# Split tokens and split weights in tiles that begin at many different byte offsets

## The chip, the cores and the metric

The kernel runs on 1 core of one Trainium2 chip. The metric is device time in microseconds (us) of one execution, from the program's start to its end. Before the change it is 2146.31 us, the median of 3 runs (2145.34 to 2146.55).

## What is computed

The reference is the trunk of an encoder with two layers, 256 tokens and a model width of 2048, all in float32. Cut to what matters here, one layer is

```
h = rms_norm(x, ln1_g)
qa, ka, va, qb, kb, vb = split(h @ w_in)          # 2048 -> 4608
oa = neighborhood_attention(qa, ka, va, rpb)      # 8 heads of 128
ob = windowed_gqa_sink(qb, kb, vb, sink)          # 8 heads, 2 key heads
x = x + concat(rms_norm(oa), rms_norm(ob)) @ w_out
h2 = rms_norm(x, ln2_g)
u = depthwise_conv(h2 @ w_up)                     # 2048 -> 2 * 5632
x = x + (silu(u[:5632]) * u[5632:]) @ w_down      # 5632 -> 2048
```

Nearly all of the arithmetic is in the four large products with w_in, w_out, w_up and w_down.

## The kernel before, in words

**Products of split numbers.** TensorE multiplies in a 32-bit format that is rounded (fp32r in the profile). To keep float32 accuracy each number is written as the sum of a rounded high part and a low part (`split`, lines 95 to 104: ScalarE writes the high part in L98 or L101, VectorE the rest in L99 or L102), and three partial products are added: high by high, low by high, high by low. So tokens and weights lie in SBUF as pairs of tiles.

- Split tokens: `xs[k]`, k from 0 to 15, each 128 partitions by 2 parts by 256 tokens (2048 bytes in each partition), made by `prep_x` (line 115) from the residual stream; and the tiles named `mid`, of the same shape, which hold the attention outputs (line 366) and the gated activations (line 513).
- Split weights: the pair `whi`, `wlo`, each 128 by 1024 numbers (4096 bytes in each partition), made by `split_w` (line 573).

**Quanta and steps.** The weights arrive by DMA in quanta of 128 by 2048 numbers (1 MB, tile `raw`, three buffers, line 567). Each quantum is two steps of 1024 columns. The loop at the end of the function (lines 662 to 668) goes through all steps in order: it splits the weights four steps ahead (SPLIT_AHEAD), then runs the matmuls of the present step. `whi` and `wlo` have five buffers each, under one name each, in rotation.

**Two forms of product.** For w_in, w_out and w_down (`three`, line 382) the split tokens are the stationary operand (loaded into the array, 128 columns, 512 bytes in each partition) and 512 columns of `whi` or `wlo` stream past. A step has 12 such matmuls: 8 that stream `whi`, 4 that stream `wlo`. The profile names them `mm<-whi,mid`, `mm<-wlo,mid`, `mm<-whi,xs` and `mm<-wlo,xs`: the streamed tile comes first, the stationary one second. For w_up (`two`, line 377) the weights are stationary and the tokens stream: one matmul of 512 columns (both parts of a token tile) against `whi`, `mm<-xs,whi`, and one of 256 columns (the high part) against `wlo`, `mm<-xs,wlo`. A step has 8 such pairs. Every matmul has its own weight load, listed as LDWEIGHTS on PEld, and the load for the next matmul runs beside the present one.

Between them stand smaller float32 matmuls and transposes of the attention, on tiles `qT`, `kT`, `v_a`, `v_b`, `qtok`, `prob`, `prob_a`, and of the residual stream `x`.

**Order.** The Tile framework's scheduler orders each engine's instructions; the split of a step can be done as soon as its `raw` has landed and the buffer that it writes has been read for the last time.

Of the kernel before, what the change touches and what calls it, by code (L numbers as in the profile page):

```python
# [12 lines left out]
F32R = mybir.dt.float32r  # L13
# [5 lines left out]
P = 128  # L19
L = 2  # L20
T = 256
# [20 lines left out]
LOAD_AHEAD = 3  # L42
SPLIT_AHEAD = 4
AHEAD_PRIO = 40


@with_exitstack
def encoder_kernel(
# [7 lines left out]
    wp = ctx.enter_context(tc.tile_pool(name="wp", bufs=2))  # L56
    act = ctx.enter_context(tc.tile_pool(name="act", bufs=1))
# [37 lines left out]
    def split(hi, lo, src, scale=None):  # L95

        if scale is None:
            high = nc.scalar.activation(hi, src, AF.Copy)  # L98
            nc.vector.tensor_sub(lo, src, hi.bitcast(F32))  # L99
        else:  # L100
            high = nc.scalar.activation(hi, src, AF.Copy, scale=scale)  # L101
            nc.vector.scalar_tensor_tensor(lo, src, scale, hi.bitcast(F32),  # L102
                                           op0=ALU.mult, op1=ALU.subtract)
        return high
# [7 lines left out]
    xs = {}  # L112
    st = {}

    def prep_x(l, which, k, src):

        xs[k] = act.tile([P, 2, T], F32R, name=f"xs{k}")
        split(xs[k][:, 0], xs[k][:, 1], src, ln_g[:, which, l, k:k + 1])

    def square_x(nb):  # L120
# [7 lines left out]
    def turn_x(l, which, nb):  # L128

        for k in range(4 * nb, 4 * nb + 4, 2):  # L130
            ps = psum.tile([P, 2, T], F32, name="S", bufs=2)
            for j in range(2):
                for tt in range(TT):
                    nc.tensor.transpose(ps[:, j, tt * P:(tt + 1) * P], x[:, tt, (k + j) * P:(k + j + 1) * P], ident)  # L134
            for j in range(2):
                prep_x(l, which, k + j, ps[:, j, :])
# [305 lines left out]
    def add_x(nb, ps, r=None):  # L442
        xv = x[:, :, nb * 512:(nb + 1) * 512]
        if r is None:
            nc.vector.tensor_add(xv, xv, ps)  # L445
        else:
            for tt in range(TT):
                nc.vector.scalar_tensor_tensor(xv[:, tt], ps[:, tt], r[:, tt:tt + 1], xv[:, tt],
                                               op0=ALU.mult, op1=ALU.add)
# [17 lines left out]
    def whole_x(q, l, which, nb, ps, r=None):  # L467

        with tc.high_priority(offset=4 * AHEAD_PRIO if nb == NB - 1 else 0):
            add_x(nb, ps, r)  # L470
# [7 lines left out]
    def q_up(l, f, u):  # L478
        def body(q, half, hi, lo):
# [8 lines left out]
            if u == 1 and half == 1:  # L488
                with tc.high_priority(offset=4 * AHEAD_PRIO if f == NF - 1 else 0):
                    glu(l, f, ps)  # L490
        return body

    def glu(l, f, ps):
        ux = halo[f % 2]
        r = T // GRID_W
        t = work.tile([P, 2, T], F32, name="prob", bufs=2)
        nc.scalar.activation(t, ps[:, :, 0], AF.Copy)  # L497
        nc.vector.tensor_add(t, t, ps[:, :, 1])  # L498
        nc.vector.tensor_mul(ux[:, :, r:r + T], t, st["r2"][:, None, :].to_broadcast([P, 2, T]))  # L499

        nc.gpsimd.tensor_copy(ux[:, :, 1:r], ux[:, :, T:T + r - 1])  # L501
        nc.gpsimd.tensor_copy(ux[:, :, T + r:T + 2 * r - 1], ux[:, :, r + 1:2 * r])
        y = work.tile([P, 2, T], F32, name="pT", bufs=4)
        for j in range(2):
            c = j * NF + f
            w0, w1, w2, b = (par["conv"][:, l, i, c:c + 1] for i in range(4))
            nc.scalar.activation(y[:, j, :], ux[:, j, r:r + T], AF.Identity, scale=w1, bias=b)  # L507
            for w, o in ((w0, 0), (w2, 2 * r)):
                nc.vector.scalar_tensor_tensor(y[:, j, :], ux[:, j, o:o + T], w, y[:, j, :],  # L509
                                               op0=ALU.mult, op1=ALU.add)  # L510
        nc.scalar.activation(t[:, 0, :], y[:, 0, :], AF.Silu)  # L511
        nc.vector.tensor_mul(t[:, 1, :], t[:, 0, :], y[:, 1, :])  # L512
        gs[f] = act.tile([P, 2, T], F32R, name="mid", bufs=16)
        split(gs[f][:, 0], gs[f][:, 1], t[:, 1, :])
# [22 lines left out]
    for l in range(L):  # L537
# [7 lines left out]
        f = 0  # L545
# [17 lines left out]
    raw, hl, left, loads, highs = {}, {}, {}, {}, {}  # L563

    def load(q, parts=1):
        if q < len(quanta):
            raw[q] = wp.tile([P, 2048], F32, name="raw", bufs=3)
            left[q] = 2
            m = 2048 // parts
            for j in range(parts):  # L570
                loads[q] = nc.sync.dma_start(out=raw[q][:, j * m:(j + 1) * m], in_=quanta[q][0][:, j * m:(j + 1) * m])  # L571

    def split_w(s, parts=1):
        if s < len(steps):
            q, half = steps[s]
            hl[s] = tuple(wp.tile([P, 1024], F32R, name=t, bufs=SPLIT_AHEAD + 1) for t in ("whi", "wlo"))
            m = 1024 // parts
            for j in range(parts):
                with tc.high_priority(offset=AHEAD_PRIO if s >= KD // 2 else 0):
                    highs[s] = split(*(t[:, j * m:(j + 1) * m] for t in hl[s]),  # L580
                                     raw[q][:, half * 1024 + j * m:half * 1024 + (j + 1) * m])
            left[q] -= 1
            if left[q] == 0:
                del raw[q]
                load(q + LOAD_AHEAD)
# [11 lines left out]
    def first_x(i):  # L597
        for j in range(2):
            prep_x(0, 0, 2 * i + j, xT[i][:, j, :])
# [45 lines left out]
    for i in range(SPLIT_AHEAD):  # L645
        first_x(i)
        split_w(i, 2 if i == 0 else 1)
# [14 lines left out]
    for s, (q, half) in enumerate(steps):  # L662
        if s + SPLIT_AHEAD < KD // 2:
            first_x(s + SPLIT_AHEAD)
        split_w(s + SPLIT_AHEAD)
        quanta[q][1](q, half, *hl.pop(s))
        for f, args in side.pop((q, half), []):
            f(*args)
# [83 lines left out]
```

## Time and profile before

| what | value |
|---|---|
| median of 3 runs | 2146.31 us |
| the profiled execution, its own time | 2145.35 us |
| its span, first to last instruction | 2143.6 us |
| mean granted TensorE clock | 0.999 |
| busy: PE, PEld, DVE, ACT, POOL | 2135.8, 1812.2, 1462.1, 1141.5, 66.0 us |
| matmuls | 10896 |
| HBM traffic | 185 GB/s over the span |

Engines are called PE (matmuls of TensorE), PEld (its weight loads), DVE (VectorE), ACT (ScalarE), POOL (GpSimd) and SP (SyncE, which issues the DMAs). A row of a group reads: line, engine, operation, tile written and tiles read, shapes, count | busy us, mean ns of one | idle time just before them, and what ended it. Matmuls are pipelined: the recorded length of one overlaps the start of the next, so lengths don't add up to the span.

### The profile page before, as it was taken

How to read it: one execution, taken by the hardware profiler on the slowest of the kernel's cores; microseconds unless marked ns; L12 is line 12 of the kernel's file. 1: busy time of each engine (PE TensorE's matmuls, PEld its weight loads, DVE VectorE, ACT ScalarE, POOL GpSimd, SP SyncE). 2: the span in 40 equal slices, each digit the busy share in tenths (PEclk: the TensorE clock that was granted, in tenths of full speed). 3: DMA queues.
4: the chain of work that ended last, by engine and by line, in shares of the span. 5: the costliest groups of instructions: out<-in, count | busy, mean ns of one | idle time of the engine just before them, and what ended most of it. 6: DMA issues, size and time to landing. Idle time of an engine off the chain costs nothing.

```text
span 2143.6 us, 28784 instructions
## 1 busy us (share of the span) xinstructions
PE 2135.8 (100%) x10896; PEld 1812.2 (85%) x10896; DVE 1462.1 (68%) x2291; ACT 1141.5 (53%) x1651; POOL 66.0 (3%) x215
## 2 busy tenths in 40 slices
PE   9999999999999999999999999999999999999999
PEld 7888888888888888888888888888888888888887
DVE  7777667775677567657756866677756775776575
ACT  7466556554455355535655665555544553555453
POOL 0000000000000000000000000000000000000000
PEclk9999999999999999999999999999999999999999
DMA  9544555555555555555555344555555555555553
GB/s 340 194 141 167 175 177 177 188 186 197 183 190 191 190 190 179 194 195 178 195 178 196 138 170 164 177 177 184 189 197 180 193 188 187 194 178 196 191 183 137
DMA packets 60555, 397.89 MB, mean 186 GB/s; under 512 B 7296, under 2 KB 9344, under 8 KB 13440
## 3 DMA queue, kind: packets, MB, share of 16 engines
q1 hardware_dynamic: 59840, 395.00, 53.5%
q8 instruction: 85, 1.39, 0.3%
q10 hardware_dynamic: 576, 1.05, 0.2%
q14 instruction: 54, 0.44, 0.1%
HBM read 393.93 MB, written 2.10 MB: 185 GB/s over the span
## 4 chain that ended last, share of the span: by engine, by line
PE 99%; DMA 0%; SPq 0%; DVE 0%; ACT 0%; DVEq 0%; issue 0%
PE mm L80 95%; PE pv L80 1%; PE S L80 1%; PE tr L286 1%; PE S L134 0%; PE tr L347 0%; PE tr L80 0%; DMA raw<-in_w_in 0%; PE tr L342 0%; PE tr L339 0%; DVE x L533 0%; ACT whi L98 0%; DVEq L747 0%; SPq L571 0%; SPq L64 0%
## 5 line engine op out<-in xcount | busy, mean ns | idle before, releaser
L99 DVE TENSOR_TENSOR wlo<-raw,whi 128x1024 fp32r<-128x1024 f32 (+1 forms) x737 | 901.8, 1224 | 558.4 <-ACT whi L98 522.3
L98 ACT ACTIVATE whi<-raw 128x1024 fp32r<-128x1024 f32 (+1 forms) x737 | 779.8, 1059 | 885.8 <-PE mm L80 682.4
L80 PE MATMUL mm<-xs,whi 128*128 128x512 f32 x2816 | 995.0, 399 | 0.0
L80 PE MATMUL mm<-xs,wlo 128*128 128x256 f32 x2816 | 790.9, 281 | 0.0
L80 PEld LDWEIGHTS mm<-xs,whi 128*128 128x128 f32 x2816 | 528.9, 188 | 131.4
L80 PEld LDWEIGHTS mm<-xs,wlo 128*128 128x128 f32 x2816 | 531.9, 189 | 0.7
L80 PE MATMUL mm<-whi,mid 128*128 128x512 f32 x1920 | 481.0, 391 | 0.0
L80 PEld LDWEIGHTS mm<-whi,mid 128*128 128x128 f32 x1920 | 358.0, 188 | 72.8
L80 PE MATMUL mm<-whi,xs 128*128 128x512 f32 x1152 | 297.7, 396 | 2.4 <-ACT whi L98 2.4
L80 PE MATMUL mm<-wlo,mid 128*128 128x512 f32 x960 | 259.3, 390 | 0.0
L80 PEld LDWEIGHTS mm<-whi,xs 128*128 128x128 f32 x1152 | 215.6, 189 | 47.2 <-ACT whi L98 2.9
L80 PEld LDWEIGHTS mm<-wlo,mid 128*128 128x128 f32 x960 | 180.1, 188 | 37.2
L80 PE MATMUL mm<-wlo,xs 128*128 128x512 f32 x576 | 162.0, 396 | 0.0
L509 DVE SCALAR_TENSOR_TENSOR pT<-halo,conv,pT 128x256 f32<-128x256 f32 x352 | 146.4, 475 | 0.1
L80 PEld LDWEIGHTS mm<-wlo,xs 128*128 128x128 f32 x576 | 107.6, 189 | 21.4
L507 ACT ACTIVATE pT<-halo,conv 128x256 f32<-128x256 f32 x176 | 95.0, 587 | 0.0
L499 DVE TENSOR_TENSOR halo<-prob,r 128x512 f32<-128x512 f32 x88 | 60.9, 692 | 2.7
L501 POOL COPY halo<-halo 128x6 f32<-128x6 f32 x88 | 17.7, 201 | 1454.7 <-DVE halo L499 1454.7
L498 DVE TENSOR_TENSOR prob<-prob,mm 128x512 f32<-128x512 f32 x88 | 59.9, 680 | 0.0
L445 DVE TENSOR_TENSOR x<-x,mm 128x1024 f32<-128x1024 f32 x28 | 34.2, 1221 | 35.2 <-PE mm L80 35.2
L497 ACT ACTIVATE prob<-mm 128x512 f32<-128x512 f32 x88 | 51.0, 579 | 0.0
L512 DVE TENSOR_TENSOR prob<-prob,pT 128x256 f32<-128x256 f32 x88 | 36.9, 419 | 1.5 <-ACT prob L511 1.5
(129 smaller groups left out, 840.9 us busy)
## 6 DMA issues: line engine op xcount, KB each, us to landing
raw<-in_w_up SPq DMA_DIRECT2D x176, 1024.0 KB, 4.8
raw<-in_w_down SPq DMA_DIRECT2D x88, 1024.0 KB, 4.8
raw<-in_w_in SPq DMA_DIRECT2D x71, 1024.0 KB, 4.8
raw<-in_w_out SPq DMA_DIRECT2D x32, 1024.0 KB, 4.8
bias<-in_bias SPq DMA_DIRECT2D x16, 160.0 KB, 3.0
x<-in_x SPq DMA_DIRECT2D x4, 512.0 KB, 9.9
out<-x SPq DMA_DIRECT2D x8, 256.0 KB, 2.1
mid<-in_xT ACTq DMA_DIRECT2D x4, 256.0 KB, 5.4
```

What stands on the lines that cost most here:

```text
L80: nc.tensor.matmul(ps, lhsT, rhs, start=start, stop=stop, skip_group_check=True)
L98: high = nc.scalar.activation(hi, src, AF.Copy)
L99: nc.vector.tensor_sub(lo, src, hi.bitcast(F32))
L286: nc.tensor.transpose(ps[:, j, tt * P:(tt + 1) * P], qn[tt][:, p + j, :], ident)
L445: nc.vector.tensor_add(xv, xv, ps)
L497: nc.scalar.activation(t, ps[:, :, 0], AF.Copy)
L498: nc.vector.tensor_add(t, t, ps[:, :, 1])
L499: nc.vector.tensor_mul(ux[:, :, r:r + T], t, st["r2"][:, None, :].to_broadcast([P, 2, T]))
L501: nc.gpsimd.tensor_copy(ux[:, :, 1:r], ux[:, :, T:T + r - 1])
L507: nc.scalar.activation(y[:, j, :], ux[:, j, r:r + T], AF.Identity, scale=w1, bias=b)
L509: nc.vector.scalar_tensor_tensor(y[:, j, :], ux[:, j, o:o + T], w, y[:, j, :], op0=ALU.mult, op1=ALU.add)
L512: nc.vector.tensor_mul(t[:, 1, :], t[:, 0, :], y[:, 1, :])
```

## The change

The change alters only where tiles lie. Each of the sixteen `xs[k]` is cut from a longer allocation (8 more numbers for each k, so 32 bytes times k), and the five buffers of `whi` and of `wlo` become five tiles each, with names of their own, that begin 0, 8, 4, 16 and 2 numbers (0, 32, 16, 64 and 8 bytes) into allocations that are longer by as much. No tile changes its shape and no instruction is added or taken away.

```
+OFFSETS = (0, 8, 4, 16, 2)
...
-        xs[k] = act.tile([P, 2, T], F32R, name=f"xs{k}")
+        xs[k] = act.tile([P, 2 * T + 8 * k], F32R, name=f"xs{k}")[:, 0:2 * T].rearrange("p (i t) -> p i t", i=2)
...
-            hl[s] = tuple(wp.tile([P, 1024], F32R, name=t, bufs=SPLIT_AHEAD + 1) for t in ("whi", "wlo"))
+            n = s % (SPLIT_AHEAD + 1)
+            hl[s] = tuple(wp.tile([P, 1024 + OFFSETS[n]], F32R, name=f"{t}{n}", bufs=1)[:, OFFSETS[n]:]
+                          for t in ("whi", "wlo"))
```

Where the tiles begin, as the built program lays them out, in bytes modulo 512 (every slice that is loaded as weights begins a multiple of 512 bytes further on, so it has the same place):

| tiles | before | after |
|---|---|---|
| whi, five buffers | all 384 | 384, 416, 464, 64, 136 |
| wlo, five buffers | all 384 | 384, 448, 496, 128, 168 |
| xs0 to xs15 | all 384 | 192, 192, 224, 288, 384, 0, 160, 352, 64, 320, 96, 416, 256, 128, 32, 480 |
| mid, sixteen buffers | all 384 | all 192 |
| raw | all 384 | all 384 |

Of the other tiles, `x` begins at 128, `ident` at 384, `prob_a` at 64, `v_a`, `v_b`, `qT`, `kT` at 448, `qtok` at 192, `prob` at 480 and `pT` at 224 before.

Because a buffer now belongs to a step by its number (s modulo 5) and not by rotation, the scheduler's order differs in a few places. The first is on ACT where layer 1 goes over to w_up, just after the row normalisation is evacuated into `r2`. The names are tiles with their running numbers: `whi_3208` is the high part of one step, `whi_3229` of the next, and in the changed kernel the digit behind `whi` is the buffer. Before:

```order
L98 ACTIVATE whi_3168<-raw_3006 128x1024
L151 ACTIVATE r2_3146<-pv_3144 128x256
L98 ACTIVATE whi_3208<-raw_3040 128x1024
L98 ACTIVATE whi_3229<-raw_3040 128x1024
L497 ACTIVATE prob_3190<-mm_3060 128x512
L98 ACTIVATE whi_3251<-raw_3107 128x1024
```

And in the changed kernel, at the same place of the same engine:

```order
L100 ACTIVATE whi1_3168<-raw_3006 128x1024
L153 ACTIVATE r2_3146<-pv_3144 128x256
L100 ACTIVATE whi3_3229<-raw_3040 128x1024
L100 ACTIVATE whi2_3208<-raw_3040 128x1024
L499 ACTIVATE prob_3190<-mm_3060 128x512
L100 ACTIVATE whi4_3251<-raw_3107 128x1024
```

The two halves of one quantum have changed places; VectorE's low parts of the two change places with them.

The second is on ACT where the last w_up step of a layer gives way to the last w_down chunk; `prob_8867` and `mid_8882` belong to the last gated activation, which the matmuls after it read. Before:

```order
L507 ACTIVATE pT_8873<-halo1_111,conv_464 128x256 x2
L98 ACTIVATE whi_8937<-raw_8807 128x1024
L511 ACTIVATE prob_8867<-pT_8873 128x256
L98 ACTIVATE whi_8955<-raw_8849 128x1024
L98 ACTIVATE mid_8882<-prob_8867 128x256
L98 ACTIVATE whi_8971<-raw_8849 128x1024
L98 ACTIVATE whi_8990<-raw_8906 128x1024
L98 ACTIVATE whi_9033<-raw_8906 128x1024
```

And in the changed kernel:

```order
L509 ACTIVATE pT_8873<-halo1_111,conv_464 128x256 x2
L100 ACTIVATE whi1_8971<-raw_8849 128x1024
L513 ACTIVATE prob_8867<-pT_8873 128x256
L100 ACTIVATE whi4_8937<-raw_8807 128x1024
L100 ACTIVATE mid_8882<-prob_8867 128x256
L100 ACTIVATE whi0_8955<-raw_8849 128x1024
L100 ACTIVATE whi3_9033<-raw_8906 128x1024
L100 ACTIVATE whi2_8990<-raw_8906 128x1024
```

The high part of a step two further on (8971) now stands ahead of 8937 and 8955, and 9033 ahead of 8990. The same stands at the end of layer 2. On PE one matmul of the last w_down chunk moves by eight places within its neighbours at each of the two layer ends; SP's loads keep their order.

## The prediction

> **What bounds the kernel now.** I read the page first, then the list of who waited for whom, then the groups by shape, then single matmuls by cutting the groups to a stretch of a few nanoseconds. The page says that the core is a row of matmuls from end to end:
>
> ```profile
> span 2143.6 us, 28784 instructions
> PE 2135.8 (100%) x10896; PEld 1812.2 (85%) x10896; DVE 1462.1 (68%) x2291; ACT 1141.5 (53%) x1651; POOL 66.0 (3%) x215
> PE 99%; DMA 0%; SPq 0%; DVE 0%; ACT 0%; DVEq 0%; issue 0%
> ```
>
> The last line is the chain that ended last. The waits of PE amount to two at the start, 3.5 us in all, while ScalarE waits for PE to release the buffers of the split weights:
>
> ```profile
> PE mm L80 <- ACT whi L98: 2.4, 2, 1.4
> PE pv L80 <- DVE halfpi L76: 1.1, 1, 1.1
> ACT whi L98 <- PE mm L80: 682.4, 488, 4.0
> ```
>
> So loads, splits and evacuations are hidden, and only what makes a matmul itself longer or shorter can move the end. The groups by shape, with their counts (mean ns of one is the second number behind the bar):
>
> ```profile
> L80 PE MATMUL mm<-xs,whi 128*128 128x512 f32 x2816 | 995.0, 399 | 0.0
> L80 PE MATMUL mm<-xs,wlo 128*128 128x256 f32 x2816 | 790.9, 281 | 0.0
> L80 PE MATMUL mm<-whi,mid 128*128 128x512 f32 x1920 | 481.0, 391 | 0.0
> L80 PE MATMUL mm<-whi,xs 128*128 128x512 f32 x1152 | 297.7, 396 | 2.4 <-ACT whi L98 2.4
> L80 PE MATMUL mm<-wlo,mid 128*128 128x512 f32 x960 | 259.3, 390 | 0.0
> L80 PE MATMUL mm<-wlo,xs 128*128 128x512 f32 x576 | 162.0, 396 | 0.0
> ```
>
> A recorded length overlaps the next start. Eight matmuls in a row of the timeline show by how much:
>
> ```profile
> 900.85 1.98 PE L80 MATMUL mm<-whi,mid 128*128 128x512 f32 x8
> ```
>
> They take 1.98 us from the first start to the last end; less one length of 0.389 that is 1.59 us for seven starts, 227 ns each. So I use lengths only for differences: one ns more in the length is about one ns more to the next start.
>
> The question is then whether a matmul's length depends on where its operands begin. All the split tiles begin at 384 modulo 512, so the big groups can't tell. But each time the stream of large matmuls gives way to attention or transposes, the weight load beside the last large matmul reads another tile, which begins elsewhere. Cut to the first 20 ns of five such matmuls, the groups show which load runs beside each:
>
> ```profile
> L80 PEld LDWEIGHTS pv<-pT,v_b 128*128 128x128 f32 x1 | 0.2, 187 | 0.0
> L347 PEld LDWEIGHTS tr<-ident,prob 128*128 128x128 f32 x1 | 0.1, 139 | 0.0
> L339 PEld LDWEIGHTS tr<-ident,prob_a 128*128 128x128 f32 x1 | 0.1, 140 | 0.0
> L134 PEld LDWEIGHTS S<-ident,x 128*128 128x128 f32 x1 | 0.1, 139 | 0.0
> L286 PEld LDWEIGHTS tr<-ident,qtok 128*128 128x128 f32 x1 | 0.1, 138 | 0.0
> ```
>
> and cut to their later part, in the same order, how long those five large matmuls were (at 158, 121, 208, 304 and 164 us; I took ones that end at least 15 large matmuls in a row, since a few after an interruption vary):
>
> ```profile
> L80 PE MATMUL mm<-whi,xs 128*128 128x512 f32 x1 | 0.4, 388 | 0.0
> L80 PE MATMUL mm<-whi,xs 128*128 128x512 f32 x1 | 0.4, 392 | 0.0
> L80 PE MATMUL mm<-wlo,xs 128*128 128x512 f32 x1 | 0.4, 400 | 0.0
> L80 PE MATMUL mm<-wlo,mid 128*128 128x512 f32 x1 | 0.4, 393 | 0.0
> L80 PE MATMUL mm<-whi,xs 128*128 128x512 f32 x1 | 0.4, 392 | 0.0
> ```
>
> The undisturbed length, with the load at the stream's own place, is this, from a cut at 900 us:
>
> ```profile
> L80 PE MATMUL mm<-wlo,mid 128*128 128x512 f32 x1 | 0.4, 389 | 0.0
> ```
>
> The streams begin at 384. The load begins ahead of it, modulo 512, by 64 bytes for v_b, 96 for prob, 192 for prob_a, 256 for x, 320 for qtok. So the lengths over 389 are about 0, 3, 11, 4 and 3 ns. Prob and prob_a are transposed by the same operation into the same PSUM tile and differ in nothing but their place, and yet 392 stands against 400. I read this as a price of reading weights and stream at different places.
>
> **The change part by part.**
>
> *The order on ACT and PE.* ScalarE splits four steps ahead, and a step of 12 matmuls lasts 12 x 0.227 = 2.7 us. At the layer's end the delayed split 8937 needs its buffer, whose last reader is the group of eight at 1036.48, and it is itself read by the four and eight matmuls after the pair at 1046.91:
>
> ```profile
> 1036.48 1.98 PE L80 MATMUL mm<-whi,mid 128*128 128x512 f32 x8
> 1042.60 3.56 PE L80 MATMUL mm<-whi,mid 128*128 128x512 f32 x15
> 1046.91 0.39 PE L80 MATMUL mm<-whi,mid 128*128 128x512 f32 x1
> ...
> 1039.46 0.40 ACT L98 ACTIVATE mid<-prob 128x256 fp32r<-128x256 f32 x1
> ...
> L98 ACT ACTIVATE whi<-raw 128x1024 fp32r<-128x1024 f32 x735 | 778.6, 1060 | 884.4 <-PE mm L80 682.4 <-issue 131.8 <-ACT pT L507 58.1
> ```
>
> The buffer is free at 1038.5 and the split takes 1.06 us, so it is done 7 us before it is read. The activation behind it in the queue, mid_8882, ends at 1039.9 now and would end no more than 0.2 us later; it is first read by the eighth of the fifteen matmuls from 1042.60, at 1044.2. The swapped halves at the start of w_up have the same lead. I take 0 for all of it, and 1 us at most each way. If that cover were gone, each place would cost PE a wait of one split, 1.06 us.
>
> *Writes into the new places.* They cost PE nothing: VectorE and ScalarE are idle for a third and a half of the span. They are also indifferent to the place so far as rows tell: adds of one shape into prob (480) and into qtok (192) take 680 and 685 ns.
>
> ```profile
> L498 DVE TENSOR_TENSOR prob<-prob,mm 128x512 f32<-128x512 f32 x88 | 59.9, 680 | 0.0
> L278 DVE TENSOR_TENSOR qtok<-qtok,tq 128x512 f32<-128x512 f32 x8 | 5.5, 685 | 0.0
> ```
>
> *Matmuls with mid* (1920 + 960). The loads now begin at 192, the streams at five places each. With straight lines between the measured points (0 at 0 and 64, 3 at 96, 11 at 192, 4 at 256, 3 at 320, and, chosen, 0 from 384 on), the distances 320, 288, 240, 128 and 56 bytes of the whi buffers give 3.0, 3.5, 5.8, 5.7 and 0 ns, mean 3.6; 320, 256, 208, 64 and 24 of the wlo buffers give 3.0, 4.0, 9.3, 0 and 0, mean 3.3. Two thirds of the first and one third of the second are 3.5 ns, times 2880 matmuls 10.0 us.
>
> *Matmuls of w_in* (1152 + 576). Sixteen places of xs against the same streams: the mean by the same lines is 3.1 ns, times 1728 it is 5.4 us.
>
> *Matmuls of w_up* (2816 pairs). Here the lengths at equal places already are not 389: three cuts in a row at 600 us give 395, 403 and 398, a beat of three pairs that goes on through the stage.
>
> ```profile
> L80 PE MATMUL mm<-xs,whi 128*128 128x512 f32 x1 | 0.4, 395 | 0.0
> L80 PE MATMUL mm<-xs,whi 128*128 128x512 f32 x1 | 0.4, 403 | 0.0
> L80 PE MATMUL mm<-xs,whi 128*128 128x512 f32 x1 | 0.4, 398 | 0.0
> ```
>
> The mean of 399 is 10 ns over the undisturbed 389, so this stage pays already what reads in all relations to each other cost. If places only shuffle that, it stays: I take 0. The bounds: a gain of 10 ns in 2816 pairs, 28 us, if the beat went; a loss of the lines' mean of 3.0 ns in each of the 5632, 17 us, if it came on top. That one weight buffer in five begins at an odd 8 bytes, no row prices; I leave it inside these bounds.
>
> *The sum.* 10.0 + 5.4 + 0 + 0 = 15.4 us. The profiled execution took 2145.35 us, 1.75 more than its span and 0.96 less than the median of the runs shown: 2145.35 + 15.4 = 2161 us. Three of the points behind the line are transposes; should a transpose add 3 ns by itself, the two terms shrink to 3.7 + 2.5 = 6.2, so 2151.5. With w_up's 17 on top it is 2178. So the forecast's own range is 2151 to 2178.
>
> **The rivals.**
>
> *The place doesn't matter* (0.22). The extra of the five matmuls would then be something of the transposes, and the time stays 2145 to 2146. For it: in the float32 matmuls of attention, S reads both operands at 448 and pv one at 448 and one at 224, with the same length.
>
> ```profile
> L80 PE MATMUL S<-kTb,qT 128*128 128x256 f32 x64 | 15.8, 379 | 0.0
> L80 PE MATMUL pv<-pT,v_b 128*128 128x256 f32 x64 | 16.4, 379 | 0.0
> ```
>
> Against it: these don't stream fp32r, and prob against prob_a. The Trainium skill, TensorE: Matmul & The Clock Gate, under Step-by-step: what each phase is for, says that TensorE has two independent read ports into SBUF, so that loading the next weights doesn't take bandwidth from the running matmul. By that rule the answer is this rival's; the 400 against 392 doesn't agree with it.
>
> *The beat of w_up goes* (0.14), a gain. Equal places would be the bad case of the streamed xs, where whi and wlo slices and token tiles of 512 and 256 columns keep meeting; spread, they meet seldom. Price: -28 us on w_up, +15 on the rest, 2133 us. It decides for a faster kernel once more than 15 of the 28 us go. For it: 395 to 403 at equal places; against: the w_down matmuls have equal places too, and 389.
>
> *All meeting goes* (0.08). Equal places would cost every matmul something, and spread ones nothing. The S row's 379, with as large a load beside it, is the nearest to a matmul without it: 10 ns in the 4608 matmuls of the other products and 20 in the 2816 of w_up are 46 + 56 = 102 us, 2043 us. Against it: not one of the five matmuls at other distances was shorter than 388.
>
> **How the numbers follow.** Forecast 0.56, the rivals 0.22, 0.14 and 0.08. The range takes in the forecast's own range, no effect, and the beat's end: 2130 to 2182; outside are the last rival and about 0.08 of the forecast's and the beat's ends. A measurement of this kernel tells 0.2%, 4.3 us, from no change. Faster by more: 0.14 + 0.08 = 0.22; within: 0.22; slower: 0.56.
>
> **What would show it.** In the changed profile the four groups of 389 to 396 ns with mid and xs as weights should stand some 3 ns higher, and those with mid should differ by buffer: 64 bytes or less apart unchanged, 208 to 240 bytes apart the longest, near 395. The pair of w_up should stay near 399 and 281 in the mean, no longer in a beat of three. PE should still wait for nothing behind the start. I am wrong if the w_down groups stay at 390 (no effect) or fall, or if the w_up groups move by more than 5 ns, since the term of 0 is the least supported one.

## The result and the profile after

The changed kernel takes 2161.64 us, the median of 4 runs (2160.73 to 2162.95), against 2146.35 us (4 runs, 2145.34 to 2146.55). The ratio is 1.0073, with a 95% interval of 1.0055 to 1.009: slower, by some 15 us. Its profiled execution took 2162.15 us, its span is 16.8 us longer than before. The page's head, and the chain that ended last:

```profile
span 2160.4 us, 28779 instructions
PE 2153.1 (100%) x10896; PEld 1815.2 (84%) x10896; DVE 1461.7 (68%) x2291; ACT 1142.0 (53%) x1651; POOL 68.2 (3%) x215
PE 99%; DMA 0%; SPq 0%; DVE 0%; ACT 0%; DVEq 0%; issue 0%
```

The list of waits, as far as PE stands in it:

```profile
PE mm L82 <- ACT whi L100: 1.9, 2, 1.1
PE pv L82 <- DVE halfpi L78: 1.1, 1, 1.1
```

PE still waits for nothing behind the start, so the 16.8 us are in the matmuls. The groups (busy us, mean ns of one):

```profile
L82 PE MATMUL mm<-xs,whi 128*128 128x512 f32 x2816 | 987.1, 395 | 0.0
L82 PE MATMUL mm<-xs,wlo 128*128 128x256 f32 x2816 | 789.9, 281 | 0.0
L82 PE MATMUL mm<-whi,mid 128*128 128x512 f32 x1920 | 491.7, 397 | 0.0
L82 PE MATMUL mm<-whi,xs 128*128 128x512 f32 x1152 | 302.7, 401 | 1.9 <-ACT whi L100 1.9
L82 PE MATMUL mm<-wlo,mid 128*128 128x512 f32 x960 | 264.5, 395 | 0.0
L82 PE MATMUL mm<-wlo,xs 128*128 128x512 f32 x576 | 165.1, 402 | 0.0
```

Against the same rows of before, the two groups with mid rose by 10.7 + 5.2 = 15.9 us, the two of w_in by 5.0 + 3.1 = 8.1 us, and the two of w_up fell by 7.9 + 1.0 = 8.9 us. That is 15.1 of the 16.8 us; added up from start to start (from the start of one matmul to the start of the next) over the trace's records, which takes out the modelled ends, it is 16.7, 8.2 and -8.0, so 16.9 us.

In the timeline of PE, a w_down step is the time from one group of eight to the next. Before:

```profile
501.65 1.98 PE L80 MATMUL mm<-whi,mid 128*128 128x512 f32 x8
504.37 1.98 PE L80 MATMUL mm<-whi,mid 128*128 128x512 f32 x8
```

After, three steps in a row (their numbers make them the steps of weight buffers 3, 4 and 0):

```profile
507.39 2.02 PE L82 MATMUL mm<-whi,mid 128*128 128x512 f32 x8
510.18 2.04 PE L82 MATMUL mm<-whi,mid 128*128 128x512 f32 x8
512.99 2.04 PE L82 MATMUL mm<-whi,mid 128*128 128x512 f32 x8
515.80 2.02 PE L82 MATMUL mm<-whi,mid 128*128 128x512 f32 x8
```

A step took 2.72 us, 227 ns a matmul. It takes 2.79, 2.81 and 2.81 us now, and 2.79 for the other two buffers: 6 to 7.5 ns more in each of its twelve matmuls on average, whatever the buffer.

### The profile page after: what moved, and what is told of

It reads as the page before. It is cut to its first block, busy times and chain, and to the rows that moved or that the text cites. A ratio compares the mean times of both kernels' runs of the same rounds, so it can differ in the third digit from the quotient of the medians.

```text
span 2160.4 us, 28779 instructions
## 1 busy us (share of the span) xinstructions
PE 2153.1 (100%) x10896; PEld 1815.2 (84%) x10896; DVE 1461.7 (68%) x2291; ACT 1142.0 (53%) x1651; POOL 68.2 (3%) x215
## 4 chain that ended last, share of the span: by engine, by line
PE 99%; DMA 0%; SPq 0%; DVE 0%; ACT 0%; DVEq 0%; issue 0%
PE mm L82 95%; PE pv L82 1%; PE S L82 1%; PE tr L288 1%; PE S L136 0%; PE tr L349 0%; DMA raw<-in_w_in 0%; PE tr L82 0%; PE tr L344 0%; PE tr L341 0%; DVE x L535 0%; ACT whi L100 0%; DVEq L751 0%; SPq L573 0%; SPq L66 0%
## 5 line engine op out<-in xcount | busy, mean ns | idle before, releaser
L82 PE MATMUL mm<-whi,mid 128*128 128x512 f32 x1920 | 491.7, 397 | 0.0
L82 PE MATMUL mm<-whi,xs 128*128 128x512 f32 x1152 | 302.7, 401 | 1.9 <-ACT whi L100 1.9
L82 PE MATMUL mm<-wlo,mid 128*128 128x512 f32 x960 | 264.5, 395 | 0.0
L514 DVE TENSOR_TENSOR prob<-prob,pT 128x256 f32<-128x256 f32 x88 | 36.9, 419 | 1.6 <-ACT prob L513 1.6
```

Source lines behind the costliest of these rows:

```text
L82: nc.tensor.matmul(ps, lhsT, rhs, start=start, stop=stop, skip_group_check=True)
```

## The experiments

The theory on trial was the prediction's: a matmul is lengthened by the distance, from the place of the stream to the place of the loaded weights, by something like its line. The rivals were that place doesn't matter, and, once the result was there, that any unequal place costs the same. Distances below are place of the weights less place of the stream.

### The order alone

The names of the buffers as in the change, without any offset.

```
+            n = s % (SPLIT_AHEAD + 1)
+            hl[s] = tuple(wp.tile([P, 1024 + OFFSETS[n]], F32R, name=f"{t}{n}", bufs=1)[:, OFFSETS[n]:]
...
+OFFSETS = (0, 0, 0, 0, 0)
```

> Five named buffers each for whi and wlo as in the change, but all at 384 modulo 512, and xs not spread: only the scheduler's order of the change is left. Relative place (a price when weights that load and the stream beside them begin at different places): 2146 us, within 2 us of the kernel before. Absolute place (a price for beginning elsewhere than at 384): the same, 2146 us. Order or fixed buffers: about 2161 us, the time of the change.

Measured: 2145.96 us, ratio 1.0 (0.9991 to 1.001). The groups of w_up and w_down are those of before:

```profile
L82 PE MATMUL mm<-xs,whi 128*128 128x512 f32 x2816 | 995.0, 399 | 0.0
L82 PE MATMUL mm<-whi,mid 128*128 128x512 f32 x1920 | 480.7, 391 | 0.0
```

The other order and the fixed buffers cost nothing. All of the change's effect is in the places.

### Everything moved together

A constant that lies ahead of the pools grows, so that all the split tiles begin at 64 instead of 384; they keep their places to one another.

```
-            nc.scalar.activation(const.tile([P, 1], F32, name="junk"), halfpi, AF.Copy)
+            nc.scalar.activation(const.tile([P, 56], F32, name="junk")[:, 0:1], halfpi, AF.Copy)
```

> The kernel before with 192 bytes of unused space ahead of the pool of raw, whi, wlo, mid and xs: every one of them begins at 64 instead of 384, still all at one place. Relative place: 2146 us, w_down matmuls at 389 ns and the w_up pair in its beat at 399 and 281. Absolute place: 2150 to 2161 us, w_down matmuls at 393 ns or more.

Measured: 2140.29 us, ratio 0.9974 (0.9964 to 0.9983). The w_down groups stay at their lengths:

```profile
L80 PE MATMUL mm<-whi,mid 128*128 128x512 f32 x1920 | 481.0, 391 | 0.0
L80 PE MATMUL mm<-wlo,mid 128*128 128x512 f32 x960 | 259.3, 390 | 0.0
```

So their length goes by relative places, not by the place itself. Neither forecast had a gain. It is 5 us, all in w_up, and there in one stretch of each layer, the 13 w_up tiles ahead of the first w_down chunk. The same group at 400 to 440 us and at 600 to 640 us of this kernel:

```profile
L80 PE MATMUL mm<-xs,whi 128*128 128x512 f32 x116 | 40.3, 394 | 0.0
L80 PE MATMUL mm<-xs,whi 128*128 128x512 f32 x115 | 40.7, 399 | 0.0
```

Equal work at equal distances runs in one of two rhythms, 394 or 399 ns, and keeps it through a stretch. From start to start they are 347 and 353 ns a pair. Before had the slow one in all its eight stretches.

### The weights' part alone

The change without the longer `xs` allocations; mid and xs then all begin at 192.

```
-        xs[k] = act.tile([P, 2 * T + 8 * k], F32R, name=f"xs{k}")[:, 0:2 * T].rearrange("p (i t) -> p i t", i=2)
+        xs[k] = act.tile([P, 2, T], F32R, name=f"xs{k}")
```

> Only the split weights spread, with xs left at one place (they and mid land at 192, the weights at 384, 416, 464, 64, 136 and 384, 448, 496, 128, 168). Relative place: w_down as in the change (mean lengths 397 and 395), the w_in groups near these too, so about 8 to 10 us from w_in and 17 from mid, and w_up some 8 us less as in the change: 2161 to 2166 us. If the gain in w_up comes from the spread of xs: 2168 to 2174 us.

Measured: 2158.4 us, ratio 1.0059 (1.0044 to 1.0074).

```profile
L82 PE MATMUL mm<-xs,whi 128*128 128x512 f32 x2816 | 982.4, 393 | 0.0
L82 PE MATMUL mm<-whi,mid 128*128 128x512 f32 x1920 | 491.7, 397 | 0.0
L82 PE MATMUL mm<-whi,xs 128*128 128x512 f32 x1152 | 302.7, 400 | 2.1 <-ACT whi L100 2.1
L82 PE MATMUL mm<-wlo,mid 128*128 128x512 f32 x960 | 264.5, 395 | 0.0
L82 PE MATMUL mm<-wlo,xs 128*128 128x512 f32 x576 | 165.4, 402 | 0.0
```

The whole price of w_down is there (+15.9 us), and that of w_in too (+8.4). w_up gains more than in the full change, 14.1 us with the wlo group (790.9 to 789.4; 12.7 us from start to start), not the 8 us that the forecast took over from it, so the time lies below both forecast ranges. That the place doesn't matter is out.

### The tokens' part alone

```
-        xs[k] = act.tile([P, 2, T], F32R, name=f"xs{k}")
+        xs[k] = act.tile([P, 2 * T + 8 * k], F32R, name=f"xs{k}")[:, 0:2 * T].rearrange("p (i t) -> p i t", i=2)
```

> Only xs spread, weights and mid all at 384. Relative place: w_down stays at 391 and 390 ns as before; w_in pays some 8 us as in the change; w_up gains some 8 us as in the change: 2144 to 2148 us. If the gain in w_up comes from the spread of the weights: 2152 to 2155 us. Absolute place of mid as the cause of the w_down price: w_down as before here too.

Measured: 2144.57 us, ratio 0.9994 (0.9985 to 1.0004), no difference that can be told.

```profile
L80 PE MATMUL mm<-xs,whi 128*128 128x512 f32 x2816 | 987.2, 394 | 0.0
L80 PE MATMUL mm<-whi,mid 128*128 128x512 f32 x1920 | 481.1, 391 | 0.0
L80 PE MATMUL mm<-whi,xs 128*128 128x512 f32 x1152 | 301.6, 400 | 2.4 <-ACT whi L98 2.4
```

Two things cancel: w_up falls by 7.8 us in this group, w_in rises by 3.9 here and 2.2 in its other group (162.0 to 164.2), w_down stays. Each half of the change brings the w_up gain by itself, and the gains don't add.

### w_down by distance

Two kernels put the pairs of `mid` tiles at eight distances each from streams that all stay at 384; one step reads one pair, so each step shows one distance. The first goes by 64 bytes, the second takes 0, 8, 16, 32, 48, 96, 160 and 480 (the list and the helper of the first; the second has another list):

```
+MID = ((0, 512), (0, 512), (16, 528), (0, 512), (16, 528), (0, 512), (16, 528), (0, 512), (16, 528), (0, 512), (16, 528), (0, 512), (16, 528), (0, 512), (16, 528), (0, 528))
...
+    def mid_tile(dt):
+        n = len(mids) % 16
+        inner, size = MID[n]
+        mids.append(act.tile([P, size], dt, name=f"mid{n}", bufs=1)[:, inner:inner + 2 * T].rearrange("p (i t) -> p i t", i=2))
+        return mids[-1]
```

> Weights and xs all at 384 as before; only the mid tiles spread, in eight pairs 0, 64, 128 up to 448 bytes ahead of the streams, so that each w_down step has one distance. If the price follows the single matmuls at the transitions (the forecast's line): lengths of 389 at 0, 64, 384 and 448, about 394 at 128, 400 at 192, 393 at 256 and 392 at 320; 2154 us. If in a steady run any distance other than 0 costs about the same: 394 to 396 at all seven and 389 at 0; 2161 us. w_in and w_up as before in both.

> The same with distances 0, 8, 16, 32, 48, 96, 160 and 480 bytes. By the forecast's line: 389 at 0 to 48 and at 480, 392 at 96, 397 at 160; 2150 us. If any distance costs about the same: 394 to 396 at all but 0; 2161 us. If 8 bytes past a multiple of 16 have a price of their own, the 8-byte pair stands out over the 16-byte pair.

Measured: 2149.92 and 2160.17 us, one run each beside a before of 2145.63. Five steps in a row of the first kernel's timeline, at distances 64, 128, 192, 256 and 320:

```profile
503.23 2.03 PE L81 MATMUL mm<-whi,mid 128*128 128x512 f32 x8
...
506.03 2.02 PE L81 MATMUL mm<-whi,mid 128*128 128x512 f32 x8
...
508.82 1.99 PE L81 MATMUL mm<-whi,mid 128*128 128x512 f32 x8
...
511.58 1.99 PE L81 MATMUL mm<-whi,mid 128*128 128x512 f32 x8
...
514.31 2.03 PE L81 MATMUL mm<-whi,mid 128*128 128x512 f32 x8
...
517.11 0.39 PE L81 MATMUL mm<-whi,mid 128*128 128x512 f32 x1
```

The steps last 2.80, 2.79, 2.76, 2.73 and 2.80 us. So 256 is nearly as good as the 2.72 of before, 320 as bad as 64, and the one middle value is at 192. Of the second kernel, at distances 0, 8 and 16:

```profile
501.79 1.98 PE L81 MATMUL mm<-whi,mid 128*128 128x512 f32 x8
...
504.51 2.01 PE L81 MATMUL mm<-whi,mid 128*128 128x512 f32 x8
...
507.28 2.03 PE L81 MATMUL mm<-whi,mid 128*128 128x512 f32 x8
...
510.08 2.02 PE L81 MATMUL mm<-whi,mid 128*128 128x512 f32 x8
```

2.72, 2.77 and 2.80 us: 8 bytes already cost 4 ns a matmul, 16 cost 5 to 7. Taken over all steps from start to start, the streams of `wlo`, which come last in a step and have settled, run at 226.7 ns for 0, 226.9 for 256, 230.9 for 8, 228.9 for 192 and 228.8 for 448, and 231.7 to 235.3 for 16, 32, 48, 64, 96, 128, 160, 320, 384 and 480. The prediction's line, nothing up to 64 and most at 192, falls. What stands in its place is nearly "any unequal place costs some 6 ns", with a period of 256 bytes, free at its multiples and cheap 64 bytes below them. This holds for streams that have settled: in the changed kernel the four `wlo` streams of weight buffer 1 lie 256 bytes from their loads and yet run at 231.5 ns in the mean, behind eight streams at 288.

The second kernel's total is the one that goes with a price at any unequal place, and not the line's. The first kernel's lies below both, since 256 is free and 192 and 448 are cheap, and since w_up ran its fast rhythm in three of its eight stretches there (988.4 us in its first group against 995.0), though none of its tiles had been moved: the rhythm depends on what went before.

### w_up at one other distance

`xs` moved so that `whi` lies 224 bytes ahead of the stream and `wlo` 256.

```
+        n = 72 if k == 0 else 0
+        xs[k] = act.tile([P, 2 * T + n], F32R, name=f"xs{k}")[:, n:].rearrange("p (i t) -> p i t", i=2)
...
+            hl[s] = tuple(wp.tile([P, 1024 + m], F32R, name=f"{t}{n}", bufs=1)[:, 0:1024]
+                          for t, m in (("whi", 8), ("wlo", 120)))
```

> All whi at 384, all wlo at 416, mid at 384, all xs at 160, so that in w_up the whi load lies 224 and the wlo load 256 bytes ahead of the stream, as for buffer 1 of the run with weights only, whose pairs took 346 ns. If the distances set the pair's time: w_up at 344 to 347 ns a pair in the whole stage, 18 to 26 us less; w_in 5 to 10 us more; the 960 wlo matmuls of w_down up to 6 us more: 2126 to 2143 us. If w_up gained only because spread places break the beat: pairs at 350 or more, 2143 to 2156 us.

Measured: 2142.11 us, ratio 0.9984 (0.9975 to 0.9993).

```profile
L80 PE MATMUL mm<-xs,whi 128*128 128x512 f32 x2816 | 970.5, 388 | 0.0
L80 PE MATMUL mm<-whi,mid 128*128 128x512 f32 x1920 | 487.9, 395 | 0.0
L80 PE MATMUL mm<-wlo,mid 128*128 128x512 f32 x960 | 265.7, 397 | 0.0
```

w_up falls by 24.5 us in this group at one constant distance, so its gain needs no spreading. The rest gives most of it back: `wlo` now lies 32 bytes off mid's place, and the `whi` streams suffer too (391 to 395), though they lie at mid's place. The eight of them follow four at another distance, and in the kernel with mid by 64 bytes the matmuls that come back to distance 0 also take some six to settle.

### The rhythm set from outside

Before, with one more matmul of a single column ahead of three w_up tiles in each layer; its weights begin 320, 256 and 192 bytes ahead of 384 in layer 1, and 0, 64 and 128 in layer 2. Nothing reads its result.

```
+            if u == 0 and half == 0 and f in (13, 25, 37):
+                e = RESET[l * 3 + (f - 13) // 12]
+                mm(psum.tile([P, T], F32, name="pv", bufs=1)[:, 0:1],
+                   par["conv"].rearrange("p l i f -> p (l i f)")[:, e:e + P], ident[:, 0:1], True, True)
```

> The kernel before, all places equal, with one extra float32 matmul of one column (its result is not read) ahead of w_up tiles 13, 25 and 37 of each layer; its weights lie 320, 256 and 192 bytes (layer 1) and 0, 64 and 128 bytes (layer 2) ahead of 384. If the beat of w_up is a state that a stretch keeps from its first matmuls: some of the six stretches run at 346.7 ns a pair (lengths of about 392 and 280, no beat) and the others at 353.3; 2131 to 2143 us. If the beat belongs to equal places: all at 353.3, 2146 to 2148 us.

Measured: 2140.2 us, ratio 0.9976 (0.9966 to 0.9985), with six float32 matmuls more than before, each of which the trace lists as two. The group in the stretches behind 320 and 256, 40 us of each:

```profile
L81 PE MATMUL mm<-xs,whi 128*128 128x512 f32 x117 | 40.6, 394 | 0.0
L81 PE MATMUL mm<-xs,whi 128*128 128x512 f32 x115 | 40.7, 399 | 0.0
```

Behind 192 and 64 it is 394 and 393 as well, behind 0 and 128 it is 399. One small matmul decides 6 ns a pair in a stretch of 768 records. So the rhythm is a state that lasts, and not something of the data, the loads or the buffers of that stretch. The six came in an order in which fast and slow alternate, so this run alone doesn't tell the place of the extra weights from their order; without the extra matmul nothing alternated, all eight stretches were slow.

### w_up by distance

The weights of w_up use a piece of a longer tile, at 44 settings of high and low part, two w_up tiles each; all other products use the tile's start.

```
+UP = [(h, (h + r) % 256) for r in (0, 32, 64, 128, 224) for h in range(0, 256, 32)] + [(16, 16), (240, 0), (208, 240), (224, 16)]
...
+            hl[s] = tuple(wp.tile([P, 1088], F32R, name=t, bufs=SPLIT_AHEAD + 1)[:, d // 4:d // 4 + 1024]
+                          for t, d in zip(("whi", "wlo"), up.get(q, (0, 0))))
```

> The kernel before with split weights in tiles 64 columns longer, of which the matmuls of w_up alone use a piece that begins 0 to 252 bytes behind the tile's start, by tile pair of the hidden width: 44 settings of high and low part, each over two steps f (64 pairs of matmuls). All other tiles keep their places, except that the longer tiles put every second weight tile 256 bytes further. Theory (the price of a matmul goes by the distance of weights and stream modulo 256 bytes, w_up too): each setting has a steady length of its own; high part 224 bytes and low part 0 bytes on, which was the setting with 344.6 ns a pair in the run with the streams moved, gives 344.6 ns again, some settings lie above 353.5 ns and the worst at most 340 + 2 x 7 = 354 ns; the lines of w_down stay at 439.5 and 218.7 us in all and those of w_in at 405 us, since 256 bytes are no distance. Rival (places count modulo 512 bytes, and w_up gains by any unequal place alike): all settings but the first lie within 2 ns of 350, and w_down gets dearer by some 10 us since half of its streams lie 256 bytes off. Time by the theory 2125 to 2147 us, by the rival some 2146 - 2816 x 3.5 ns + 10 = 2146 us.

Measured: 2135.96 us, one run, beside 2146.79 before. Pairs in three of the settings, high and low part: 0 and 0, 224 and 0, 192 and 0:

```profile
L81 PE MATMUL mm<-xs,whi 128*128 128x512 f32 x23 | 8.2, 399 | 0.0
L81 PE MATMUL mm<-xs,wlo 128*128 128x256 f32 x24 | 6.6, 281 | 0.0
...
L81 PE MATMUL mm<-xs,whi 128*128 128x512 f32 x30 | 10.4, 388 | 0.0
L81 PE MATMUL mm<-xs,wlo 128*128 128x256 f32 x30 | 8.4, 280 | 0.0
...
L81 PE MATMUL mm<-xs,whi 128*128 128x512 f32 x27 | 9.3, 389 | 0.0
L81 PE MATMUL mm<-xs,wlo 128*128 128x256 f32 x28 | 7.6, 276 | 0.0
```

From start to start these are 353.4, 344.3 and 340.6 ns a pair. Over all 44 settings the mean is 349.3, the dearest 353.4 and the cheapest 340.6, which is 192 and 0. The setting of the run with `xs` moved gave its length again. None lies above 353.5 ns, where the theory had put some. The half of the weight tiles that begins 256 bytes further cost w_down nothing (481.0 and 259.3 us, as before): the period of 256 holds there too. The rival with its 2146 us falls.

Each setting ran once, behind one other. Of the 44, 15 ran at 346.5 to 346.7 ns and ten at 353.1 to 353.4, the values of the two rhythms at equal places; high and low part moved alike gave the slow value at 0, 32 and 64 bytes and the fast one at 16, 96 and 224. So for these settings the map doesn't tell what the places do from what the rhythm does. Beside w_down by distance the map says where before stood: equal places are the cheapest for w_down, and, in the rhythm it had, the dearest for w_up.

### The cheapest distance in all of w_up

```
+            d = 48 if q in ups else 0
+            hl[s] = (wp.tile([P, 1088], F32R, name="whi", bufs=SPLIT_AHEAD + 1)[:, d:d + 1024],
+                     wp.tile([P, 1024], F32R, name="wlo", bufs=SPLIT_AHEAD + 1))
...
+                    ups.add(len(quanta))
```

> The kernel before with the high parts of split weights in tiles 64 columns longer; the matmuls of w_up alone use a piece that begins 192 bytes behind the tile's start, all others the piece at the start. So the high parts of w_up begin 192 bytes (modulo 256) behind the streams' place, the low parts at it. Theory (the steady length of a pair goes by the two distances, and before was near the dearest of the table): all 2816 pairs at about 340.6 ns as in the map, 36 us less than before in w_up (995.4 to about 960 us), w_down at 658.2 and w_in near 406 us unchanged; 2108 to 2113 us. Rival (the short stretches of the map owed their length to the stretch ahead, and a long one falls back into a beat of its own): first records near 227 and 113, later ones near 231 and 117, 346.7 ns a pair or more; 2127 us or above. A second rival (a faster w_up meets what feeds it, the splits of the weights): waits of PE on the split tiles appear in the list of waits, 5 to 20 us of them; 2115 to 2130 us.

Measured: 2108.54 us (5 runs, 2108.03 to 2109.59), ratio 0.9825 (0.9812 to 0.9839). It beats both kernels.

```profile
span 2107.8 us, 28784 instructions
L80 PE MATMUL mm<-xs,whi 128*128 128x512 f32 x2816 | 958.2, 389 | 0.0
L80 PE MATMUL mm<-xs,wlo 128*128 128x256 f32 x2816 | 777.4, 276 | 0.0
```

In its timeline at 600 us the w_up pairs start 0.34 us apart, with no beat left:

```profile
599.85 0.39 PE L80 MATMUL mm<-xs,whi 128*128 128x512 f32 x1
600.08 0.28 PE L80 MATMUL mm<-xs,wlo 128*128 128x256 f32 x1
600.19 0.39 PE L80 MATMUL mm<-xs,whi 128*128 128x512 f32 x1
```

The two w_up groups fall by 36.8 + 13.5 us in busy time; from start to start it is 995.4 to 958.5 us, 36.9, and the span fell by 35.8, while w_in took 1.0 us more. The w_down groups stay at 481.0 and 259.3 us. A long stretch doesn't fall back into a beat, and PE waits for the splits no more than before:

```profile
PE mm L80 <- ACT whi L98: 1.6, 2, 1.0
```

With w_down at 226.7 ns for 512 columns, a pair of 512 and 256 columns at the same rate would be 340 (an estimate from these rows): by it, little is left to win by places.

## Why the prediction came out, point by point

*PE bounds, and only a matmul's length counts.* Right: the waits after are 1.9 and 1.1 us, at the start.

*Order and writes, 0.* Right. The order alone gave a ratio of 1.0, and a split of 1024 columns on ScalarE takes 1061 ns after, 1060 before.

*Unequal places of weights and stream lengthen a matmul.* Right, and shown by undoing and by doing parts alone: w_down rose only where its weights' or streams' places were made unequal. "The place doesn't matter" was the wrong rival. Prob against prob_a pointed the right way, though not by its order: it had 96 bytes cheap and 192 dear, and settled streams have 96 dear (235.3 ns) and 192 cheap (228.9). The rule cited for that rival (the Trainium skill, TensorE: Matmul & The Clock Gate, Step-by-step: what each phase is for) isn't borne out at unequal places: the streams of `whi` with `mid` as weights took 397 ns after against 391 before. Whether it holds for the cheapest cases, 227 and 340 ns, no run here shows, since a weight load stands beside every matmul.

*The line over the distance.* Wrong. It was drawn through single matmuls at a change of tile; a matmul that stands alone at a distance after many at another is not what a run at that distance settles to. At 64 bytes the single one showed 0 and the settled runs 6 to 7 ns; at 192 it showed 11 and they show 2; at 256, 4 and 0. So the signs by which buffers were to differ failed: buffer 4, within 64 bytes and forecast unchanged, is among the dearest at 2.81 us a step, and the four groups rose by 5 to 6 ns, not 3. Its points weren't all firm either: of the ten matmuls of the trace before that end at least 15 large ones in a row with the load of `x` beside them, five took 393 ns and five 397. And four of the five points were transposes, not three; the hedge of 3.7 + 2.5 us takes 3 ns off all four.

*The mid term, 10.0 us.* Mis-sized: 15.9 us by the groups, 16.7 from start to start. The line gave 0 to three of its ten places, which cost like the others. *The w_in term, 5.4 us.* Mis-sized for the same reason: 8.1 us.

*The w_up term, 0.* Wrong in its reason, within its bounds: -8.9 us by the groups, -8.0 from start to start. That spreading only shuffles what is paid already fails, since before was not at a mean of all relations but, in its slow rhythm, at the dearest: 353 ns a pair, where the map's mean is 349.3. In the changed kernel the pairs take 350.4 from start to start, an ordinary mix, and the beat of three is gone, as forecast: eight lengths in a row at 588.6 us are 396, 392, 398, 393, 391, 395, 392 and 396 ns. The gain is part of the rival in which the beat goes, 8.9 of its 28 us. Its bound of 28 was also too near: the best place found saves 36.9, as the `wlo` matmuls fall too (281 to 276 ns), which the bound took for untouched.

*The sum.* 15.4 us forecast, 16.8 in the span. It is close because the losses were undersized by 5.9 + 2.7 = 8.6 us, and the gain left out was 8.9. The direction and the mechanism of the losses were right; the nearness of the number is luck.

*All meeting goes, 2043 us.* Out: w_down had nothing to gain, as equal places are the cheapest of those tried, and the cheapest pair of w_up took 340 ns.

Open: why the period is 256 bytes, why the pair prefers 192 for the high part with 0 for the low one, what holds the rhythm, and how a stream's length settles over the first few matmuls at a new distance. The runs give the lengths and not the cause inside the memory or the array.

## What to carry to other kernels

Where PE is busy from end to end and every matmul brings its own weights, as here with fp32r operands (no other type was tried), the places of the two operands within 256 bytes are a tuning parameter: look for beats in the lengths of like matmuls, and measure each form of product by itself, in long runs, over the distance. Choose the place for each form (a slice offset in a longer tile is enough), rather than spread tiles, which moves each form towards its mean: a loss for the one that stood well, a gain for the one that stood badly. A price that is read from a single transition is a hint that there is one, not its size.

## What the runs showed of the hardware

- In streams that have settled, a matmul of 512 fp32r columns with a weight load beside it starts 226.7 ns after the one before when the two places are equal modulo 256 bytes, 231 ns at 8 bytes apart, 232 to 235 at 16 to 160, and 229 at 192. A stream that comes back to distance 0 takes some six matmuls to settle.
- A pair of 512 and 256 columns takes 340.6 to 353.4 ns, by the places and by a rhythm that lasts. At equal places there are two such rhythms, 347 and 353 ns, and a single one-column matmul ahead of the stretch can switch between them: with its weights at odd multiples of 64 bytes came the fast one, at even ones the slow one, three of three each (in alternating order).
- A move of all split tiles together left w_down as it was, and still moved the total by 5 us (ratio 0.9974), through the rhythm of one stretch in each layer: a change that has nothing to do with matmuls can so shift this kernel's time by more than a measurement's doubt.
